# A feed-forward norm's weight moved from the tokens to the gate and up weights, and the end of the operand's stage reordered

## The chip, the cores and the metric

The kernel runs on one core of a Trainium2 chip. The core has five engines with a queue of instructions each: TensorE (PE) for matrix products, VectorE (DVE), ScalarE (ACT) and GpSimd (POOL) for everything elementwise, and SyncE (SP), whose queue issues the DMA transfers here. The metric is the device time of one execution in microseconds (us); lower is better.

## The reference

One layer of a streaming encoder for a prompt of 1024 tokens and for 8 samples of 16 new tokens (128 rows), model width 1024, all in fp32. Two groups of eight heads attend, their outputs are normed per head and projected, and then comes the part that matters here:

```python
def rmsnorm(x, g):
    xf = x.astype(jnp.float32)
    y = xf * lax.rsqrt(jnp.mean(xf * xf, axis=-1, keepdims=True) + EPS)
    return y.astype(x.dtype) * g

    x = x + mix @ w_out
    h = rmsnorm(x, g_ffn)
    x = x + (jax.nn.silu(h @ w_gate) * (h @ w_up)) @ w_down
```

`w_gate` and `w_up` are 1024 x 2816. The weight `g_ffn` has one value for each of the 1024 columns of `h`, which are the rows of `w_gate` and `w_up`, so it may be multiplied onto either.

## The kernel before, in words

Rows of tokens are held in nine tiles of 128: tiles 0 to 7 are the prompt, tile 8 the samples. Every fp32 product is done as three products of split operands: a high part (`...h`, `hi`, made by a cast on ACT) and a low part (`...l`, `lo`, what the cast left out, made by a subtraction on DVE or POOL). So each operand costs an ACT pass and a DVE or POOL pass before PE can use it.

**The operand's stage** (lines 957 to 1126) makes the feed-forward operand. For each tile, in the order 0, 4, 1, 5, 2, 6, 8, 3, 7, `lower` (L996) multiplies the second half of the mix by the output weights and adds the first half's result on DVE (L1001); `normed_halves` (L1004) squares the two halves on ACT (L1011), makes the reciprocal root (two DVE operations, L1013 and L1014, and a power on POOL, L1015) and writes the normed row `hrow`; `spread` (L1025) turns that row with eight PE transposes (L1030) and splits the result. Tiles t and t + 4 (t < 4) are combined into the seven forms B11, B21, B22, T1 to T4 of a Strassen-like product of 2x2 blocks (seven products in place of eight); tile 8 goes into `h8`, used alone in a "decode" product (`decoded`, L1064).

In `normed_halves` DVE scales the first half by the root and by the row of the norm's weight at once (L1019). The second half goes to ACT (scale, L1021) and then POOL (times the row, L1022), but for the last two tiles, where DVE does it too (`soon`). The weight's row, `g_row`, is loaded once, copied to all 128 partitions (512 KB, L126 and L978).

**The feed-forward loop** (lines 1143 to 1226) has 22 chunks, gate and up by turns, of 256 columns each. `gate_up` (L980) issues the transfer of a chunk's 1 MB of weights into one raw buffer (L141; there is only one, so a transfer waits until the last chunk's raw values are used up). `gate_up_parts` splits them in four pieces (`whi` L159 on ACT, `wlo` L105 on POOL), `sums` (L1076) makes the four sums of blocks on DVE, and `sum_parts` (L1086) splits those. These are used one chunk later. In a chunk PE first multiplies B11 (`first`, L1069); ACT copies the result into `u` (L1073) before PE goes on adding to the same bank (`product(a, ..., True)`, L1166).

**What sets the order.** A planner orders each engine's instructions from its own estimate of their times, except where the code says that an engine takes the order of the program. In this stage PE takes the program's order from the third tile on (L1100), and from the last tile on PE, ACT and DVE do (L1112), until the block's end at L1126; POOL and SP are the planner's throughout. After that all engines are the planner's, with the raw weights' casts kept behind certain splits (L1163).

The end of the stage before: at tile 3 (`j == NT - 2`) the first gate chunk is split with DVE (L1114). At the last tile (7) comes the decode product of the first chunk (L1116), then tile 3's transposes, tile 7's norm, the sums, S1's split, the first product, tile 7's transposes and forms (L1122 to L1126).

## Time and profile before

| | us |
|---|---|
| median of 3 runs | 1719.52 (1718.66 to 1720.41) |
| the profiled execution, its own time | 1712.64 |
| its span, from first to last instruction | 1710.6 |
| PE busy | 1651.7 (97%) |
| DVE busy | 1099.0 (64%) |
| ACT busy | 807.1 (47%) |
| POOL busy | 805.7 (47%) |

The profile is one execution recorded by the hardware. Each row of a timeline gives the start, the length, the engine, the source line, the operation with its output and input, and in brackets how long the engine stood before it and what released it. L12 is line 12 of the kernel; a helper's line stands for all who call it, so `L105` is every low part that is a plain subtraction. `pt` and `ps` are PE's result banks, `hrow` the normed row, `wraw` the raw weights, `u` and `sg` the loop's results. A matmul's length overlaps with the next one's start.

### The profile page before, as it was taken

How to read it: one execution, taken by the hardware profiler on the slowest of the kernel's cores; microseconds unless marked ns; L12 is line 12 of the kernel's file. 1: busy time of each engine (PE TensorE's matmuls, PEld its weight loads, DVE VectorE, ACT ScalarE, POOL GpSimd, SP SyncE). 2: the span in 40 equal slices, each digit the busy share in tenths (PEclk: the TensorE clock that was granted, in tenths of full speed). 3: DMA queues.
4: the chain of work that ended last, by engine and by line, in shares of the span. 5: the costliest groups of instructions: out<-in, count | busy, mean ns of one | idle time of the engine just before them, and what ended most of it. 6: DMA issues, size and time to landing. Idle time of an engine off the chain costs nothing.

```text
span 1710.6 us, 27738 instructions
## 1 busy us (share of the span) xinstructions
PE 1651.7 (97%) x10308; PEld 1421.3 (83%) x10308; DVE 1099.0 (64%) x1716; ACT 807.1 (47%) x1713; POOL 805.7 (47%) x652
## 2 busy tenths in 40 slices
PE   8999999989997999898989999999999999999998
PEld 7999888989996887787868888888888878878887
DVE  6111444379889666854787666666565597798875
ACT  5323545366778777643543233333332244433673
POOL 2313301277356411322345555555555379968763
PEclk9999999999998999999999999999999999999999
DMA  5847888665369885854422222222222597722222
GB/s 193 276 151 219 275 292 293 187 187 168 116 181 277 276 266 163 252 176 169 153 82 96 96 96 95 96 93 87 86 89 95 214 367 256 257 79 111 99 98 99
DMA packets 172810, 293.49 MB, mean 172 GB/s; under 512 B 16642, under 2 KB 96258, under 8 KB 170371
## 3 DMA queue, kind: packets, MB, share of 16 engines
q1 hardware_dynamic: 172674, 291.71, 52.0%
q8 instruction: 82, 1.34, 0.3%
q14 instruction: 54, 0.43, 0.1%
HBM read 204.77 MB, written 86.90 MB: 171 GB/s over the span
## 4 chain that ended last, share of the span: by engine, by line
PE 78%; DVE 7%; DMA 6%; ACT 3%; POOL 3%; issue 2%; SPq 1%; POOLq 0%; DVEq 0%; ACTq 0%
PE ps L1058 24%; PE ps L100 6%; PE ps L101 6%; PE ps L102 6%; PE pt L1321 4%; PE pt L1058 3%; PE ps L1321 3%; PE pt L610 2%; PE pt L405 2%; PE acc L468 2%; DMA v<-sv 2%; DVE keep L114 2%; PE po L634 1%; PE sdec L427 1%; PE S L579 1%
## 5 line engine op out<-in xcount | busy, mean ns | idle before, releaser
L105 POOL TENSOR_TENSOR wlo<-wraw,whi 128x512 fp32r<-128x512 f32 (+1 forms) x119 | 211.3, 1798 | 139.7 <-ACT whi L159 138.5
L100 PE MATMUL ps<-whi,hTh 128*128 128x256 f32 x576 | 167.7, 291 | 1.3 <-ACT st L267 1.3
L101 PE MATMUL ps<-wlo,hTh 128*128 128x256 f32 x576 | 164.2, 285 | 0.0
L102 PE MATMUL ps<-whi,hTl 128*128 128x256 f32 x576 | 163.7, 284 | 0.1
L159 ACT CAST whi<-wraw 128x512 fp32r<-128x512 f32 (+1 forms) x122 | 88.6, 744 | 71.4 <-PE ps L1058 28.6
L100 PEld LDWEIGHTS ps<-whi,hTh 128*128 128x128 f32 x576 | 110.4, 192 | 7.9 <-issue 5.7
L592 POOL TENSOR_TENSOR w<-w,keep 128x127 f32<-128x127 f32 (+4 forms) x64 | 78.6, 1230 | 74.8 <-DVE keep L114 64.5
L102 PEld LDWEIGHTS ps<-whi,hTl 128*128 128x128 f32 x576 | 110.4, 192 | 0.8 <-DVE hTl L105 0.4
L101 PEld LDWEIGHTS ps<-wlo,hTh 128*128 128x128 f32 x576 | 110.5, 192 | 0.2
L614 ACT CAST wth<-pt 128x512 fp32r<-128x512 f32 (+1 forms) x192 | 84.4, 466 | 44.5 <-PE pt L610 43.9
L105 DVE TENSOR_TENSOR wtl<-pt,wth 128x512 fp32r<-128x512 f32 (+1 forms) x192 | 94.1, 513 | 14.8 <-ACT wth L614 14.7
L114 DVE TENSOR_TENSOR_SCAN keep<-keep,zero 128x128 f32<-128x128 f32 (+7 forms) x64 | 101.6, 1588 | 1.7
L610 PE MATMUL pt<-ident,w 128*128 128x128 f32 x528 | 90.4, 284 | 8.5 <-DVE wtl L105 4.4
L610 PEld LDWEIGHTS pt<-ident,w 128*128 128x128 f32 x528 | 64.2, 144 | 21.6 <-DVE wtl L105 6.0
L579 PE MATMUL S<-qk 128*128 128x384 f32 (+2 forms) x192 | 71.9, 376 | 6.5 <-ACT keep L583 4.4
L633 PE MATMUL po<-wth,vk 128*128 128x256 f32 (+1 forms) x304 | 76.5, 283 | 1.5 <-DVE wtl L105 1.2
L105 POOL TENSOR_TENSOR actl<-actr,acth 128x1024 fp32r<-128x1024 f32 (+1 forms) x22 | 61.2, 2782 | 34.2 <-DMA sr<-acts 20.7
L634 PE MATMUL po<-wtl,vk 128*128 128x256 f32 (+1 forms) x304 | 73.4, 285 | 0.0
L406 DVE COPY kT<-pt 128x512 f32<-128x512 f32 x48 | 33.0, 687 | 53.4 <-PE pt L405 49.5
L101 PE MATMUL ps<-hTl,whi 128*128 128x384 f32 x192 | 65.4, 341 | 0.0
L102 PE MATMUL ps<-hTh,wlo 128*128 128x384 f32 x192 | 65.3, 340 | 0.0
L100 PE MATMUL ps<-hTh,whi 128*128 128x384 f32 x192 | 65.3, 340 | 0.0
(441 smaller groups left out, 5292.1 us busy)
## 6 DMA issues: line engine op xcount, KB each, us to landing
draw<-in_cache_sb_k SPq DMA_DIRECT2D x32, 512.0 KB, 5.7
draw<-in_cache_sb_v SPq DMA_DIRECT2D x32, 512.0 KB, 5.7
act<-sg SPq DMA_DIRECT2D x11, 1152.0 KB
actr<-act SPq DMA_DIRECT2D x22, 576.0 KB, 9.5
wraw<-in_w_in SPq DMA_DIRECT2D x11, 1024.0 KB, 8.7
wraw<-in_w_gate SPq DMA_DIRECT2D x11, 1024.0 KB, 5.5
wraw<-in_w_up SPq DMA_DIRECT2D x11, 1024.0 KB, 5.4
v<-sv SPq DMA_DIRECT2D x36, 256.0 KB, 4.7
```

The source lines that it names most:

```text
L100: T.matmul(out, lhsT=ah, rhs=bh, start=start, stop=False)
L101: T.matmul(out, lhsT=ah, rhs=bl, start=False, stop=False)
L102: T.matmul(out, lhsT=al, rhs=bh, start=False, stop=stop)
L105: return eng.tensor_tensor(out, a, hi.bitcast(F32), op=ALU.subtract)
L114: V.tensor_tensor_scan(rev, rev, zero[:, 0:1].to_broadcast([P, n - d]), keep[:, n - d : n - d + 1], op0=ALU.mult, op1=ALU.max)
L159: A.copy(h[:, o], v[:, o])
L579: T.matmul(sc, lhsT=hd["qq"][:, qs], rhs=hd["kkh"][:, kc], start=True, stop=False)
L610: T.transpose(pt[:, (c - c0) * P : (c - c0 + 1) * P], w[:, c * P : (c + 1) * P], ident)
L614: A.copy(wth[:, ks, qs], pv)
L634: T.matmul(dst, lhsT=vs, rhs=wtl[:, kb - base, c0:c1], start=False, stop=(i == nkb - 1))
L1058: T.matmul(out, lhsT=a[x][:, k], rhs=b[y][:, k], start=(not more and k == 0 and n == 0), stop=(k == 3 and n == 2), skip_group_check=more)
L1321: T.matmul(out, lhsT=a[i][:, x, m * P : (m + 1) * P], rhs=b[j][:, x], start=(not more and x == 0 and n == 0), stop=(x == 1 and n == 2), sk ...
```

## The change

The norm's weight is loaded as a column per block of 128 (`g_in`, 8 values for each partition) right behind the two small loads of `g_out`, and no longer as a row. `gate_up` multiplies it onto the raw weights in place: eight ACT operations of 128x256 behind each chunk's transfer, in front of the split and the sums. The normed row is then only the scale by the root, both halves on ACT.

At the end of the operand's stage: the first chunk's low parts are made by POOL and not DVE; tile 3's transposes come before the decode product; that product is cut into two halves, the second one behind the first chunk's second product; the first product and the copy of its result come before S1's split; tile 7's forms are made in another order (T2, T3 and T1 first, then B22 and T4). In the first chunk, the sums of the second one are moved behind the adds of the results.

```diff
+    g_in = cst.tile([P, KT], F32, name="g_in")
...
     for i, g in enumerate((g_out_sb, g_out_cb)):
         nc.sync.dma_start(g_out[:, i * 4 : i * 4 + 4], g.rearrange("o (k p) -> p (o k)", p=P))
+    nc.sync.dma_start(g_in, g_ffn.rearrange("o (k p) -> p (o k)", p=P))
...
-    g_row = load_row(xg, g_ffn[0:1, :], "grow")
 
     def gate_up(i):
-        return ch.raw(cols((w_gate, w_up)[i % 2][0], i // 2), KT, 256)
+        v = ch.raw(cols((w_gate, w_up)[i % 2][0], i // 2), KT, 256)
+        for k in range(KT):
+            A.activation(v[:, k], v[:, k], AF.Copy, scale=g_in[:, k : k + 1])
+        return v
...
-            if i == 0 or soon:
-                V.scalar_tensor_tensor(h[:, o], x[i], r[:, 0:1], g_row[:, o], op0=ALU.mult, op1=ALU.mult)
-            else:
-                A.activation(h[:, o], x[i], AF.Copy, scale=r[:, 0:1])
-                G.tensor_tensor(h[:, o], h[:, o], g_row[:, o], op=ALU.mult)
+            A.activation(h[:, o], x[i], AF.Copy, scale=r[:, 0:1])
...
         A.copy(v, q0)
-        A.copy(B22[0][:, :, s], q1)
+        if t < NP - 1:
+            A.copy(B22[0][:, :, s], q1)
         V.tensor_tensor(t1, v, p0, op=ALU.subtract)
         V.tensor_tensor(q0, q1, v, op=ALU.subtract)
         V.tensor_tensor(v, q1, t1, op=ALU.subtract)
+        if t == NP - 1:
+            A.copy(T2[0][:, :, s], v)
+            A.copy(T3[0][:, :, s], q0)
+            A.copy(T1[0][:, :, s], t1)
+            V.tensor_tensor(p1, p1, v, op=ALU.subtract)
+            sub(V, T2[1][:, :, s], v, T2[0][:, :, s])
+            sub(V, T3[1][:, :, s], q0, T3[0][:, :, s])
+            sub(G, T1[1][:, :, s], t1, T1[0][:, :, s])
+            for f, x in ((B22, q1), (T4, p1)):
+                A.copy(f[0][:, :, s], x)
+                sub(V, f[1][:, :, s], x, f[0][:, :, s])
+            return
...
-    def decoded(w, e):
-        for k in range(KT):
+    def decoded(w, e, ks=range(KT)):
+        for k in ks:
...
             if j == NT - 2:
-                w = gate_up_parts(raw, V)
-            if j == NT - 1:
-                e = decoded(w, bank(256))
+                w = gate_up_parts(raw)
             if rows:
                 spread(*rows.pop())
-            rows.append((order[j], normed_halves(order[j], j >= NT - 2)))
+            if j == NT - 1:
+                e = decoded(w, bank(256), range(4))
+            rows.append((order[j], normed_halves(order[j])))
...
         s = sums(raw)
+        a, u2 = first(w)
         S = {1: sum_parts(1, s, V)}
-        a, u2 = first(w)
         spread(*rows.pop())
...
             product(a, quarter(w, 1, 0), B21, True)
+            if not i:
+                decoded(w, e, range(4, KT))
...
                 nxt = gate_up_parts(raw)
-                s = sums(raw)
...
             V.tensor_tensor(u3, u3, d, op=ALU.add)
+            if not i:
+                s = sums(raw)
             if more:
                 S_next = {x: sum_parts(x, s) for x in (1, 2, 0)}
```

6 lines of the change are left out of this document (1 added, 5 removed).

## The prediction, made before the changed kernel was run

> **What bounds the kernel now.** I read the page's first part, then busy time by stretches, then TensorE's timeline in the stretch where it falls short.
>
> ```profile
> span 1710.6 us, 27738 instructions
> 795.00:815.00 20.00, 15.04 (x72) 11.18 (x72) 9.06 (x18) 7.64 (x15) 6.04 (x5) 0.91 0.50 165
> 815.00:850.00 35.00, 35.00 (x175) 29.11 (x174) 26.50 (x46) 19.59 (x45) 15.14 (x14) 1.00 0.47 171
> 850.00:895.00 45.00, 39.01 (x186) 30.41 (x185) 39.94 (x62) 24.67 (x53) 22.16 (x17) 0.96 0.22 70
> 895.00:1385.00 490.00, 487.44 (x2166) 402.57 (x2165) 302.92 (x357) 156.36 (x264) 258.31 (x173) 1.00 0.32 115
> 877.60:881.00 3.40, 3.40 (x10) 2.36 (x8) 3.12 (x5) 2.10 (x5) 1.40 (x2) 0.51 0.95 298
> ```
>
> The columns after the length of a stretch are the busy times of TensorE (PE), its weight loads, VectorE (DVE), ScalarE (ACT) and GpSimd (POOL), then granted clock, DMA share and GB/s. The operand's stage runs from about 807 to 895. It is full of matmuls until 850; its end, 850 to 895, has 45 − 39.01 = 6.0 us in which PE stands. Behind it the feed-forward loop runs 490 us with PE filled, while ACT is busy for 156 us (32%) and POOL for 258 us (53%). Work put on ACT there is free unless it stops something; the change can win only the 6.0 us, and 3.40 × (1 − 0.51) = 1.7 us in which PE ran at half clock. The ten holes:
>
> ```profile
> 855.25 0.65 PE L1030 MATMUL pt<-ident,hrow 128*128 128x128 f32 x4 [0.36 <-DVE hrow L1019]
> 856.97 0.66 PE L1030 MATMUL pt<-ident,hrow 128*128 128x128 f32 x4 [1.07 <-POOL hrow L1022]
> 860.85 0.63 PE L1030 MATMUL pt<-ident,hrow 128*128 128x128 f32 x4 [0.45 <-DVE hrow L1019]
> 862.04 0.63 PE L1030 MATMUL pt<-ident,hrow 128*128 128x128 f32 x4 [0.57 <-DVE B22l L105]
> 869.43 0.50 PE L1058 MATMUL ps<-B11h,whi 128*128 128x512 f32 x1 [0.24 <-ACT B11h L1036]
> 870.15 0.50 PE L1058 MATMUL ps<-B11l,whi 128*128 128x512 f32 x1 [0.22 <-DVE B11l L105]
> 873.29 1.23 PE L1030 MATMUL pt<-ident,hrow 128*128 128x128 f32 x8 [0.35 <-DVE hrow L1019]
> 876.32 0.50 PE L1058 MATMUL ps<-B21h,whi 128*128 128x512 f32 x1 [1.81 <-ACT u L1073]
> 890.51 0.50 PE L1058 MATMUL ps<-B11h,whi 128*128 128x512 f32 x1 [0.39 <-DVE dec L1185]
> 893.40 0.50 PE L1058 MATMUL ps<-T4h,whi 128*128 128x512 f32 x1 [0.54 <-DVE u L1195]
> ```
>
> In brackets: how long PE stood, and what released it. They add up to 6.00. Four are the normed rows of tiles 6, 8 and 7 (`hrow`) coming late, one is a bank, two the split of tile 3, the longest the copy of the first product (`u`), and two lie in the first chunk, behind DVE.
>
> **The change part by part.**
>
> *The norm without its row.* Removed per tile: the DVE pass that also multiplied by the row, and for seven tiles GpSimd's pass over the other half. Added: that ACT scales both halves.
>
> ```profile
> L1022 POOL TENSOR_TENSOR hrow<-hrow,row_grow 128x512 f32<-128x512 f32 x7 | 11.4, 1635 | 3.3 <-ACT hrow L1021 3.3
> L1019 DVE SCALAR_TENSOR_TENSOR hrow<-xa,r_n,row_grow 128x512 f32<-128x512 f32 x9 | 9.9, 1097 | 1.6 <-POOL r_n L1015 1.4
> L1015 POOL TENSOR_TENSOR r_n<-r_n,nhalf 128x1 f32<-128x1 f32 x9 | 5.2, 575 | 39.5 <-DVE r_n L1014 39.5
> L105 POOL TENSOR_TENSOR wlo<-wraw,whi 128x512 fp32r<-128x512 f32 x4 | 6.4, 1632 | 1.0 <-ACT whi L159 1.0
> 1409.26 1.94 ACT L1362 ACTIVATE q<-q,g_gate 128x512 f32<-128x512 f32 x3
> L1362 ACT ACTIVATE q<-q,g_gate 128x512 f32<-128x512 f32 x16 | 11.1, 720 | 18.4 <-DMA q<-in_w_ple_gate 13.3 <-POOL actl L105 5.1
> ```
>
> (Groups give count, then total and mean busy time.) L1362 is the operation of the change, a scale by a column, on 512 elements: 0.72 alone, three in 1.94, so (1.94 − 0.72)/2 = 0.61 apart. From the reciprocal root (L1015) to the whole row it took one ACT pass and then a POOL pass, 0.72 + 1.64 = 2.4 us; it will take 0.61 + 0.72 = 1.3. DVE loses 9.9 us, and the four subtractions of the first chunk's parts besides. ACT gains eleven scalings, 11 × 0.61 = 6.7 us, where it has 15 of 35 us free. So 1.1 us comes off the path of each row. Tile 6's 0.36 + 1.07 goes to nothing. PE then reaches tile 8 earlier by 1.4, and tile 8's row and bank (0.45 + 0.57) come earlier by only about as much: I leave 0.6 of the 1.02.
>
> The four `wlo` passes, now on POOL (1.63 each), stand in the queue of the root and of T1's and T2's subtractions. A root behind one of them makes its row 1.6 late. My sum has none behind one; the rival below has two.
>
> *The end of the stage.* Tile 3's transposes move ahead of the decode product, which used to cover their wait. From the rows of the holes, the twelve matmuls of a lower product take 860.85 − 0.45 − 856.97 − 0.66 = 2.8 us, and the 24 of the decode product 869.43 − 0.24 − 862.04 − 0.63 − 2.8 − 1.23 = 2.5. PE now has only the 2.8 of tile 7's lower product while tile 3's add, squares, root and two scalings (1.3) run: a new hole, 0.5, between 0 and the 2.5 that covered it. Half of the decode product now covers tile 3's split, so 0.24 + 0.22 goes. Tile 7's row keeps its length but has half a decode less ahead of it and starts earlier by as much: 0.2 instead of 0.35.
>
> ```profile
> 875.16 0.62 ACT L1088 CAST S1h<-s 128x512 fp32r<-128x512 f32 x1 [3.93 <-DVE s L1081]
> 875.69 0.58 ACT L1073 COPY u<-ps 128x512 f32<-128x512 f32 x1
> ```
>
> Here is the longest hole: the copy of `u` stood on ACT behind the cast of S1, which waited for DVE's sums. The change exchanges them; the product was ready at about 873, so the copy ends before tile 7's transposes do: 1.81 goes to 0.2. What is late next is the last tile's T2 and S2, two forms made by DVE one after another at 0.68 each. The other half of the decode product (1.3 us), and T2 and T3 being made first, lie over that; I leave 0.5, between 0 and 1.3.
>
> *The first chunk.* The next chunk's sums go behind the adds that PE waited for; 0.39 + 0.54 shrinks to 0.1. Those sums are needed only a chunk later, and the raw buffer is let go by a few us later at most, in front of a transfer that the loop has time for.
>
> Holes after: 0 + 0.6 + 0.5 + 0 + 0.2 + 0.2 + 0.5 + 0.1 = 2.1, against 6.0: −3.9. **The clock:** the half clock began 1.3 us after the hole of 1.81. With that hole gone I take the 1.7 as gone too; bounds 0 and −1.7.
>
> [...]
>
> *Scaling the weights.* Eight passes of 128x256 in every one of 22 chunks; no such row exists.
>
> ```profile
> L159 ACT CAST whi<-wraw 128x512 fp32r<-128x512 f32 x88 | 53.0, 622 | 54.1 <-PE ps L1058 28.6 <-PE pt L102 22.1 <-DMA wraw<-in_w_gate 3.4
> L159 ACT CAST whi<-wraw 128x1024 fp32r<-128x1024 f32 x34 | 35.7, 1057 | 17.3 <-PE ps L102 7.3 <-PE ps L101 5.0 <-DMA wraw<-in_w_in 3.3
> 1012.03 0.38 SPq L141 DMA_DIRECT2D wraw<-in_w_gate  x1
> 1027.70 0.59 ACT L1073 COPY u<-ps 128x512 f32<-128x512 f32 x1
> 1029.06 0.62 ACT L159 CAST whi<-wraw 128x512 fp32r<-128x512 f32 x1 [0.24 <-PE pt L102]
> 1035.15 0.38 SPq L141 DMA_DIRECT2D wraw<-in_w_up  x1
> 1044.37 1.14 ACT L159 CAST whi<-wraw 128x512 fp32r<-128x512 f32 x2
> 1052.25 0.58 ACT L1073 COPY u<-ps 128x512 f32<-128x512 f32 x1
> 1057.19 0.39 PE L1058 MATMUL ps<-B21h,whi 128*128 128x512 f32 x1
> DMA to landing us min/median/max: 5.3/5.4/5.6
> ```
>
> 512 elements more cost 1.057 − 0.622 = 0.435, so 256 fewer take 0.22 off: 0.61 − 0.22 = 0.39 apart, 8 × 0.39 + 0.1 = 3.2 us a chunk (estimate), 70 us in all. ACT goes from 32% to about 46%. For a gate chunk the transfer lands at 1012.4 + 5.4 = 1017.8 and the scalings end at 1021; the casts waited until 1029 for a matmul anyway. For an up chunk they end at 1035.5 + 5.4 + 3.2 = 1044.1, just where its casts began. Value 0, with a cover of 8 us in the one and 0.3 in the other; if the second cover is gone, POOL's passes over the parts shift by as much, and PE uses those parts only in the following chunk. The first chunk's scalings come when ACT has little to do (795 to 815: 7.6 of 20 us) or while it works on the mix that PE waits for: 0.3, bounds 0 and +3.2.
>
> *Transfers.*
>
> ```profile
> 788.75 0.79 SPq L126 DMA_DIRECT2D row_grow<-in_g_ffn  x1
> 792.00:794.00 2.00, 2.00 (x19) 1.95 (x18) 0.69 (x1) 1.60 (x2) 1.60 (x2) 1.00 0.45 175
> 13.69 3.09 SPq L141 DMA_DIRECT2D wraw<-in_w_in  x1
> 42.30 2.00 ACT L159 CAST whi<-wraw 128x1024 fp32r<-128x1024 f32 x2
> DMA to landing us min/median/max: 8.6/9.2/9.7
> ```
>
> The row's 512 KB were issued at 788.75 and the queues were under half busy by 792 to 794, so its loss does not hasten the mix rows that PE awaits in 795 to 815: 0, bound −1.3 (512 KB at 175/0.45 = 389 GB/s). The new column is as scattered as the two small loads that landed in 9.2 us (the last row). It goes ahead of a weight transfer issued at 13.69 and not used until 42.30: 0, since even 9.2 us more would be covered.
>
> **Sum:** −3.9 − 1.7 + 0.3 = −5.3 (rounded) on the profiled execution, whose own time is 1712.64 (span 1710.6). The median of the runs is 1719.52, 6.9 above it; I carry the difference over: **1714.3**. Bounds −9 and no gain at all.
>
> **Rivals.**
>
> *The holes come back on POOL.* Two roots of tiles 6, 8 and 3 fall behind a `wlo` pass, 2 × 1.6 = 3.2 given back: 1717.5. For it: POOL's order is the planner's, and the passes follow the casts of the first chunk's parts, which it may put among these very tiles. Against it: seven passes of 1.6 left that queue.
>
> *The half clock stays.* Other holes of half a microsecond remain: −3.6, 1715.9. For it: the slow stretch has a DMA share of 0.95, and that transfer comes again, so the cause may be another than the hole. Against it:
>
> ```profile
> 855.00:860.00 5.00, 3.68 (x19) 2.98 (x20) 4.16 (x8) 3.60 (x9) 3.61 (x3) 1.00 0.42 143
> ```
>
> five us with 1.3 of holes, spread out, kept the full clock; the slow stretch follows one long hole. [...]
>
> *ACT is held by the transfer, slower.* The scalings wait at the head of ACT's queue, and the casts of S, the sigmoids and the copy of `u` stand behind them; PE and POOL wait for these. L1362 shows it: six of its waits for a transfer took 13.3 us, 2.2 each. Held 2.2 + 3.2 = 5.4 us in front of a copy of `u`, that copy would be late, since PE needs it only 1057.19 − 1052.25 − 0.58 = 4.4 us after it is made. It decides from 4.4 us on. In one chunk of two, 11 × 1.0 = 11 us: 1714.3 + 11 = 1725. Against it: the scalings end 6.7 and 8 us ahead of the copies at 1027.70 and 1052.25.
>
> [...]
>
> *The change doesn't remove the wait:* the copy of `u` moves but the scalings of tile 7, now all on ACT, hold it. That is worth at most 0.6 and lies in the forecast's range.
>
> **How the numbers follow.** Forecast 0.56, POOL 0.21, half clock 0.12, held ACT 0.11. This kernel's measurement can tell about 0.2%, 3.4 us: faster is below 1716.1, slower above 1723. Forecast (all but a few hundredths) and half the clock case give faster 0.60; POOL and the rest same 0.29; the held ACT slower 0.11. Range: from all holes and the clock gone (−7.7, 1711.8, a little more for the transfers' bound) to the first scalings' +3.2 on the POOL case, 1720.7, with a little for repeats and the row's −1.3: 1711.5 to 1721.5. The likeliest case alone: 1711.8 to 1717.
>
> **What would show it.** Right: PE idle in 850 to 895 near 2 us instead of 6, no hole behind `u` L1073, clock 1.00 through 877 to 881, eight scalings of about 0.5 in each chunk with PE full from 895 to 1385. Wrong: holes released by POOL's root; the slow clock still there; PE waits in the loop behind ACT; a longer wait for the mix at 801 to 815.

## The result, and the profile after

| | before | after |
|---|---|---|
| median beside each other, us | 1718.08 (1716.00 to 1720.41, 6 runs) | 1726.55 (1723.92 to 1733.50, 6 runs) |
| profiled execution, own time | 1712.64 | 1726.37 |
| its span | 1710.6 | 1724.5 |

The ratio is 1.0064, 95% interval 1.0049 to 1.0078: slower, outside the forecast's range. Of all the executions below one, of the kernel with the column in place and chunk 1 held, took 3281.17 us and is left out of its ratio.

The page of the changed kernel: its span, the chain of work that ended last (shares by engine, then by line), and the group of the scalings (count, busy total and mean ns, then how long ACT stood before them and for what).

```profile
span 1724.5 us, 27899 instructions
PE 65%; DVE 12%; DMA 11%; ACT 6%; POOL 4%; issue 3%; SPq 1%; POOLq 0%; ACTq 0%; DVEq 0%
PE ps L1066 12%; PE ps L101 6%; PE ps L102 6%; PE ps L103 6%; PE pt L1332 5%; PE ps L1332 4%; DMA wraw<-in_w_gate 3%; ACT wraw L979 3%; DMA wraw<-in_w_up 2%; PE pt L606 2%; PE pt L401 2%; PE acc L464 2%; DMA v<-sv 2%; PE pt L1066 1%; PE sdec L423 1%
L979 ACT ACTIVATE wraw<-wraw,g_in 128x256 f32<-128x256 f32 x176 | 72.9, 496 | 122.2 <-DMA wraw<-in_w_gate 74.9
```

The same part of the page of the kernel before.

```profile
PE 78%; DVE 7%; DMA 6%; ACT 3%; POOL 3%; issue 2%; SPq 1%; POOLq 0%; DVEq 0%; ACTq 0%
PE ps L1058 24%; PE ps L100 6%; PE ps L101 6%; PE ps L102 6%; PE pt L1321 4%; PE pt L1058 3%; PE ps L1321 3%; PE pt L610 2%; PE pt L405 2%; PE acc L468 2%; DMA v<-sv 2%; DVE keep L114 2%; PE po L634 1%; PE sdec L427 1%; PE S L579 1%
```

This is the first reading to make. Before, the loop's products were 24% of the chain. Now they are 12%, and three new links stand in it: the gate transfer 3%, the scalings 3%, the up transfer 2%. The scalings' busy time, 72.9 us, is near the 70 of the estimate; what changed is that the way through the raw weights has become part of what sets the end.

Where the time went is counted in what TensorE lost. From the first transpose of a normed row on (822.7 before, 822.8 after) I add up its work in the timeline, each matmul at what one takes start to start in the undisturbed stretches of the kernel before (0.2275 us for 512 columns, 0.118 for 256, 0.07 for 128, the mean of the loop's own; those of the normed rows, 0.109 apart, are counted at 0.07 too, alike in every kernel), and take that from the time elapsed. The lost time when so much work was done:

| after work of | place | before | after | difference |
|---|---|---|---|---|
| 45 us | the last B21 products, just ahead of T2's | 10.3 | 5.0 | −5.4 |
| 65 us | first chunk | 13.2 | 14.1 | +0.9 |
| 150 us | about the fourth chunk | 13.3 | 18.8 | +5.5 |
| 500 us | the loop's end | 12.8 | 26.8 | +14.0 |

The last row is the 13.9 us of span. The medians differ by only 8.5, and the ratio's interval stands for 8.4 to 13.4: the profiled execution of the kernel before was one of its quicker ones (1712.64, median 1718.08), and with the new column's 32 bytes the way up to the stage is some 4 us shorter (means of the first experiment below). The end of the stage gained 5.4. Between 45 and 65 that is given back (+6.3), the first chunks take 4.6 more, and the steady loop, priced at nothing, 8.5. "A pair" is, below, the time from one copy of `u` to the second one after it, one gate and one up chunk: 43.77 in the kernel before, from the third pair to the end of the loop.

The holes of TensorE in the changed kernel from 850 to 945 (timeline; in brackets how long PE stood and what released it), and the granted clock there (windows: length, busy time of PE, PEld, DVE, ACT, POOL, granted clock, DMA share, GB/s).

```profile
859.26 1.27 PE L1025 MATMUL pt<-ident,hrow 128*128 128x128 f32 x8 [0.30 <-ACT hrow L1017]
863.92 1.27 PE L1025 MATMUL pt<-ident,hrow 128*128 128x128 f32 x8 [0.59 <-ACT hrow L1017]
877.27 0.49 PE L1066 MATMUL pt<-T2h,S1h 128*128 128x512 f32 x1 [2.76 <-ACT T2h L1045]
878.08 0.47 PE L1066 MATMUL pt<-T2l,S1h 128*128 128x512 f32 x1 [0.32 <-DVE T2l L106]
885.20 0.51 PE L1066 MATMUL ps<-T3h,S2l 128*128 128x512 f32 x1 [1.83 <-DVE S2l L106]
937.14 0.50 PE L1066 MATMUL ps<-T4h,whi 128*128 128x512 f32 x1 [1.46 <-DVE u L1204]
941.27 0.50 PE L1066 MATMUL ps<-B22h,S3h 128*128 128x512 f32 x1 [0.87 <-DVE u L1206]
```

```profile
850.00:895.00 45.00, 39.19 (x182) 31.06 (x181) 32.75 (x51) 30.73 (x65) 20.10 (x17) 0.92 0.20 66
878.00:882.00 4.00, 3.92 (x11) 3.14 (x12) 1.23 (x2) 4.00 (x10) 1.30 (x1) 0.61 0.00 0
886.00:889.00 3.00, 3.00 (x8) 2.33 (x8) 3.00 (x3) 0.00 (x0) 3.00 (x3) 0.50 0.00 0
```

The holes of the normed rows are 0.30 and 0.59, and the hole of 1.81 behind the copy of `u` is gone. In its place stands one of 2.76 ahead of T2's first product, one of 1.83 ahead of S2's low part, and half clock behind each. The timelines of SP and ACT show what T2 waited for:

```profile
870.29 0.38 SPq L137 DMA_DIRECT2D wraw<-in_w_up  x1
875.40 1.30 ACT L979 ACTIVATE wraw<-wraw,g_in 128x256 f32<-128x256 f32 x3 [2.95 <-DVE pt L1048]
876.61 0.60 ACT L1045 CAST T2h<-t 128x512 fp32r<-128x512 f32 x1
```

Three scalings of the second chunk's weights stand ahead of the cast of T2. The code writes them later; the planner moved them up. The row names a result of DVE (L1048) that they don't read, ready at the same moment; what they needed is their transfer, which took 5.0 from issue to landing. T2's values were there from 874.61 on (DVE's L1043), so ACT stood 0.8 for the transfer and worked 1.2 on the scalings while T2 waited. They could go there because their transfer was issued at 870.29, 6.1 us earlier than before (876.36), now that chunk 0's sums and parts let the raw tile go earlier.

And the loop. One pair, 1045 to 1090: the transfers' issues on SP, the scalings, the casts and the last readers of the raw tile on ACT, POOL and DVE.

```profile
1045.17 0.38 SPq L137 DMA_DIRECT2D wraw<-in_w_up  x1
1050.45 3.31 ACT L979 ACTIVATE wraw<-wraw,g_in 128x256 f32<-128x256 f32 x8 [4.27 <-DMA wraw<-in_w_up]
1054.70 2.30 ACT L155 CAST whi<-wraw 128x512 fp32r<-128x512 f32 x4
1056.91 6.86 POOL L106 TENSOR_TENSOR wlo<-wraw,whi 128x512 fp32r<-128x512 f32 x4
1065.94 1.78 DVE L1091 TENSOR_TENSOR s<-wraw,s 128x512 f32<-128x512 f32 x1
1067.74 0.38 SPq L137 DMA_DIRECT2D wraw<-in_w_gate  x1
1072.90 3.31 ACT L979 ACTIVATE wraw<-wraw,g_in 128x256 f32<-128x256 f32 x8 [7.28 <-DMA wraw<-in_w_gate]
1081.19 0.63 ACT L1145 ACTIVATE tmp<-u 128x512 f32<-128x512 f32 x1 [3.19 <-DVE u L1214]
1083.24 0.63 ACT L1145 ACTIVATE tmp<-u 128x512 f32<-128x512 f32 x1 [0.42 <-DVE u L1216]
1083.78 2.17 ACT L155 CAST whi<-wraw 128x512 fp32r<-128x512 f32 x4
1084.46 5.50 POOL L106 TENSOR_TENSOR wlo<-wraw,whi 128x512 fp32r<-128x512 f32 x4 [0.75 <-ACT whi L155]
1089.98 0.38 SPq L137 DMA_DIRECT2D wraw<-in_w_up  x1
```

Read it as a cycle. The gate transfer is issued at 1067.74, when the last sum (1065.94 + 1.78) has read the up weights; the up transfer at 1089.98, when the last low part (1084.46 + 5.50) has read the gate's. The way from one up transfer to the next is 44.81: two landings, 5.28 and 5.16; two sets of scalings, 3.31 each; and 27.8 of casts, low parts, sums and what they queue behind. There is one raw tile, so this is a ring, and a pair cannot be shorter than it. I call it the ring from here on. The 27.8 is not work of a fixed length. The gate's scalings end at 1076.21, but its casts start at 1083.78: ACT first does what had come to stand behind the scalings in its queue, and two sigmoids among it wait for adds to `u` on DVE (the rows of 1081.19 and 1083.24), which stand behind sums of the scaled weights. In the timelines of ACT, DVE and POOL nothing on the whole way round was released by PE.

### The profile page after: what moved, and what is told of

The parts are those of the page before. It is cut to its first block, busy times and chain, and to the rows that moved or that the text cites. A ratio compares the mean times of both kernels' runs of the same rounds, so it can differ in the third digit from the quotient of the medians.

```text
span 1724.5 us, 27899 instructions
## 1 busy us (share of the span) xinstructions
PE 1661.7 (96%) x10308; PEld 1418.5 (82%) x10308; DVE 1110.4 (64%) x1702; ACT 874.4 (51%) x1900; POOL 807.1 (47%) x648
## 4 chain that ended last, share of the span: by engine, by line
PE 65%; DVE 12%; DMA 11%; ACT 6%; POOL 4%; issue 3%; SPq 1%; POOLq 0%; ACTq 0%; DVEq 0%
PE ps L1066 12%; PE ps L101 6%; PE ps L102 6%; PE ps L103 6%; PE pt L1332 5%; PE ps L1332 4%; DMA wraw<-in_w_gate 3%; ACT wraw L979 3%; DMA wraw<-in_w_up 2%; PE pt L606 2%; PE pt L401 2%; PE acc L464 2%; DMA v<-sv 2%; PE pt L1066 1%; PE sdec L423 1%
## 5 line engine op out<-in xcount | busy, mean ns | idle before, releaser
L106 POOL TENSOR_TENSOR wlo<-wraw,whi 128x512 fp32r<-128x512 f32 (+1 forms) x123 | 216.7, 1787 | 145.7 <-ACT whi L155 144.6
L979 ACT ACTIVATE wraw<-wraw,g_in 128x256 f32<-128x256 f32 x176 | 72.9, 496 | 122.2 <-DMA wraw<-in_w_gate 74.9
L610 ACT CAST wth<-pt 128x512 fp32r<-128x512 f32 (+1 forms) x192 | 84.3, 465 | 43.8 <-PE pt L606 43.2
L106 DVE TENSOR_TENSOR wtl<-pt,wth 128x512 fp32r<-128x512 f32 (+1 forms) x192 | 94.2, 513 | 14.8 <-ACT wth L610 14.6
L155 ACT CAST whi<-wraw 128x512 fp32r<-128x512 f32 (+1 forms) x122 | 84.6, 738 | 19.6 <-DMA wraw<-in_w_in 8.6
L1090 DVE TENSOR_TENSOR s<-wraw 128x512 f32<-128x512 f32 x22 | 26.0, 1182 | 61.7 <-ACT wraw L979 34.7
```

What stands on the lines that cost most here:

```text
L106: return eng.tensor_tensor(out, a, hi.bitcast(F32), op=ALU.subtract)
L155: A.copy(h[:, o], v[:, o])
L610: A.copy(wth[:, ks, qs], pv)
L979: A.activation(v[:, k], v[:, k], AF.Copy, scale=g_in[:, k : k + 1])
```

## The experiments

Columns: the median; its ratio to the kernel before beside it; PE's lost time after 45, 65, 150 and 500 us of work, as above; and a pair in the steady loop (in brackets the least and the greatest, where they lie far apart). The expectations speak of "the stage's end" and "the loop" by three marks: first transpose of a normed row, first product of B11, first product with the down weights into `pt`. By these the kernel before has 46.7 and 493.0, the changed one 44.6 and 509.7; those two stand last.

| kernel | median | ratio (95%) | lost after 45 / 65 / 150 / 500 | a pair | stage / loop |
|---|---|---|---|---|---|
| before | – | 1 | 10.3 / 13.2 / 13.3 / 12.8 | 43.77 | 46.7 / 493.0 |
| changed | 1726.55 | 1.0064 (1.0049 to 1.0078) | 5.0 / 14.1 / 18.8 / 26.8 | 44.9 | 44.6 / 509.7 |
| changed, once more | 1727.92 | 1.0056 (1.0037 to 1.0075) | 5.1 / 14.2 / 19.6 / 27.9 | 45.0 | 44.6 / 510.6 |
| 32 unused bytes | 1718.84 | 1.0011 (1.0000 to 1.0022) | 10.5 / 13.7 / 15.0 / 19.9 | 44.41 | 47.1 / 499.8 |
| changed, 64 bytes | 1735.03 | 1.0100 (1.0083 to 1.0118) | 4.7 / 14.1 / 20.5 / 32.5 | 45.4 | 44.1 / 515.4 |
| old order, weights scaled | 1719.78 | 1.0017 (1.0006 to 1.0027) | 6.7 / 8.4 / 10.8 / 19.1 | 44.9 | 44.5 / 501.9 |
| new order, row on the tokens | 1723.50 | 1.0035 (1.0020 to 1.0050) | 10.5 / 12.4 / 14.7 / 14.2 | 43.77 | 50.2 / 491.2 |
| changed, column in place | 1734.30 | 1.0113 (1.0091 to 1.0135) | 4.7 / 14.0 / 20.3 / 31.4 | 45.3 | 44.1 / 514.2 |
| ... and chunk 1 held | 1731.43 | 1.0086 (1.0061 to 1.0111) | 4.5 / 6.1 / 14.6 / 25.5 | 45.3 | 44.2 / 508.4 |
| old order, column in place | 1728.44 | 1.0077 (1.0056 to 1.0098) | 6.2 / 7.8 / 11.8 / 23.2 | 45.3 | 44.0 / 506.1 |
| changed, no scalings | 1714.25 | 0.9994 (0.9977 to 1.0011) | 4.5 / 11.1 / 11.1 / 10.8 | 43.77 | 43.9 / 493.6 |
| column in place, sums held | 1736.89 | 1.0117 (1.0090 to 1.0144) | 4.7 / 12.3 / 16.9 / 34.0 | 45.9 (44.3 to 47.2) | 44.1 / 516.8 |
| ... and chunk 1 held | 1736.30 | 1.0107 (1.0091 to 1.0124) | 4.5 / 6.1 / 15.4 / 33.5 | 45.9 (44.4 to 47.2) | 44.1 / 516.6 |
| both held, column as changed | 1724.56 | 1.0046 (1.0027 to 1.0065) | 5.1 / 7.1 / 16.0 / 29.8 | 45.0 | 44.6 / 512.5 |
| half the scalings | 1721.80 | 1.0022 (1.0008 to 1.0037) | 4.5 / 10.0 / 15.7 / 15.4 | 43.77 | 43.9 / 498.2 |
| new order, scalings on DVE | 1725.45 | 1.0050 (1.0034 to 1.0066) | 4.5 / 13.3 / 18.9 / 19.8 | 43.9 | 44.2 / 502.7 |
| old order, scalings on DVE | 1726.02 | 1.0052 (1.0031 to 1.0072) | 6.2 / 10.9 / 20.3 / 20.9 | 43.9 | 43.9 / 503.9 |
| old order, ACT and DVE | 1716.78 | 1.0005 (0.9993 to 1.0017) | 6.0 / 8.0 / 13.2 / 12.7 | 43.77 | 44.0 / 495.9 |
| new order, ACT and DVE, chunk 1 held | 1715.58 | 0.9992 (0.9979 to 1.0004) | 4.5 / 6.3 / 12.5 / 12.2 | 43.77 | 44.0 / 494.9 |
| changed, chunk 1 held | 1723.03 | 1.0034 (1.0019 to 1.0050) | 5.2 / 7.1 / 14.3 / 23.1 | 45.0 | 44.7 / 505.7 |

The stretch up to the operand's stage, which no kernel changes but for 32 bytes of place, ended between 819.0 and 832.1 in these profiles; so spans and profiled times are not compared below, only lost times and medians. "In place" is explained where it first comes up.

### Does the place of the column matter, by itself?

In the loop of the changed kernel the products of the T forms with the sums took longer one by one. First suspect: the column's 32 bytes for each partition move everything that is laid out behind the constants. The kernel before, with 32 bytes that nobody reads:

```diff
     g_out = cst.tile([P, KT], F32, name="g_out")
+    pad = cst.tile([P, KT], F32, name="pad")
+    V.memset(pad, 0.0)
```

> The kernel before, with nothing added but 32 unused bytes per partition, allocated where the change puts its column and set to zero once. Theory 1 (place in memory): all that is allocated on the left behind it moves by 32 bytes, and the products of the loop whose one operand lies left (T1, T2, T3, B22) and whose other lies right (S0 to S3) start 0.234 us apart and not 0.227, median length 396 ns and not 389: 96 in two chunks, 0.7 us, some 7 us over the loop, so about 1725 and 0.4% slower. Rival (the slower pace comes from ScalarE's added writes to the same memory, or from the run): 389 ns, loop as before, ratio 1.000.

And the changed kernel with 64 bytes in place of 32:

```diff
-    g_in = cst.tile([P, KT], F32, name="g_in")
+    g_in = cst.tile([P, 16], F32, name="g_in")[:, :KT]
```

> The changed kernel, its column given 64 bytes per partition and not 32. Theory 1 (place in memory): the offset that the kernel before had comes back (modulo 64), the mixed products go back to 389 ns, 7 us less than the changed kernel, about 1719. Rival (ScalarE's work slows them, or 32 bytes more move them as far again): 396 ns or another length, about 1726.

One line's instructions, of the kernel before, with 32 unused bytes, and as changed (least, median and greatest ns; first and last start):

```profile
L1058 PE MATMUL pt<-T2h,S1h x88: 389/389/562, 880.6 to 1344.1; 128*128 128x512 f32 x88
```

```profile
L1060 PE MATMUL pt<-T2h,S1h x88: 389/395/495, 877.4 to 1348.5; 128*128 128x512 f32 x88
```

```profile
L1066 PE MATMUL pt<-T2h,S1h x88: 393/396/628, 877.3 to 1358.5; 128*128 128x512 f32 x88
```

The place matters: 32 unused bytes alone give the longer products, a pair of 44.41 and 7.1 us more lost by the loop's end (19.9 against 12.8). 64 bytes restore the pace in part (392 for these products, 388 for those of T2h with S1l), and that kernel was slower still.

The median rose by only 0.11% (0.00 to 0.22), some 2 us. The profiles of all the kernels of the table show where the rest is: with the 32 bytes the way up to the stage is shorter. The first transpose of a normed row starts at 819.0 to 825.6 in the six kernels that have them (mean 822.4) and at 822.7 to 832.1 in the thirteen that have the old place (mean 826.8; with 64 bytes 826.9). It shows early: the 901st matmul, the same in all of them, starts at 134.0 to 134.5 in the six and at 135.0 to 135.6 in the thirteen. So by these means the place gives back ahead of the stage some 4 of the 7 us that it takes in the loop, and the profile of the kernel before, at 822.7, is the earliest of its thirteen. What in that stretch gets faster, no run shows.

### The two halves of the change, apart

The weights scaled, but all in the order of before:

```diff
-        return ch.raw(cols((w_gate, w_up)[i % 2][0], i // 2), KT, 256)
+        v = ch.raw(cols((w_gate, w_up)[i % 2][0], i // 2), KT, 256)
+        for k in range(KT):
+            A.activation(v[:, k], v[:, k], AF.Copy, scale=g_in[:, k : k + 1])
+        return v
...
+            A.activation(h[:, o], x[i], AF.Copy, scale=r[:, 0:1])
```

> The norm's weight on the gate and up weights alone; the end of the stage in the order of before, first parts on VectorE, decode product whole. Theory 2 (ScalarE held by the transfers): the scalings wait for the weights as in the changed kernel (about 120 us in all, holes behind VectorE's additions in the first four chunks and 0.3 us in each second chunk after), so the loss is all here: 1725 to 1732. Rival (the new order is what loses): 1719 or less.

The new order, with the row on the tokens as before:

```diff
-        for k in range(KT):
-            A.activation(v[:, k], v[:, k], AF.Copy, scale=g_in[:, k : k + 1])
...
-            A.activation(h[:, o], x[i], AF.Copy, scale=r[:, 0:1])
+            if i == 0 or soon:
+                V.scalar_tensor_tensor(h[:, o], x[i], r[:, 0:1], g_row[:, o], op0=ALU.mult, op1=ALU.mult)
+            else:
+                A.activation(h[:, o], x[i], AF.Copy, scale=r[:, 0:1])
+                G.tensor_tensor(h[:, o], h[:, o], g_row[:, o], op=ALU.mult)
```

> The new order at the end of the stage alone; the norm keeps its row, no scaling of weights, no column. Theory 2: no loss in the loop (458 us from the first copy of u to the last but for its start), T2 not delayed by scalings, so the end of the stage wins 3 to 5 us: about 1714. Rival (the new order puts T2 and S2 late by itself): holes of 2.8 and 1.8 us ahead of T2 and S2 stay, 1718 to 1722.

TensorE's holes at the end of the stage, first with the weights scaled in the old order, then with the new order alone (timelines).

```profile
873.03 1.27 PE L1030 MATMUL pt<-ident,hrow 128*128 128x128 f32 x8 [0.61 <-ACT hrow L1022]
874.63 0.50 PE L1058 MATMUL ps<-B21h,whi 128*128 128x512 f32 x1 [0.33 <-ACT u L1073]
879.19 0.50 PE L1058 MATMUL pt<-T2l,S1h 128*128 128x512 f32 x1 [0.87 <-POOL T2l L106]
```

```profile
862.00 0.66 PE L1031 MATMUL pt<-ident,hrow 128*128 128x128 f32 x4 [1.76 <-DVE hrow L1020]
864.35 1.11 PE L1031 MATMUL pt<-ident,hrow 128*128 128x128 f32 x4 [1.70 <-POOL hrow L1023]
874.63 1.32 PE L1031 MATMUL pt<-ident,hrow 128*128 128x128 f32 x8 [1.89 <-DVE hrow L1020]
```

And POOL's timeline of the latter: a root (L1016) behind two of the low parts.

```profile
857.12 2.54 POOL L105 TENSOR_TENSOR wlo<-wraw,whi 128x512 fp32r<-128x512 f32 x2 [2.57 <-ACT whi L159]
859.62 0.54 POOL L1016 TENSOR_TENSOR r_n<-r_n,nhalf 128x1 f32<-128x1 f32 x1
```

Scaling the weights, without any new order, already takes the hole behind `u` from 1.81 to 0.33 and the lost time after 45 us of work from 10.3 to 6.7: with the row off the tokens, tile 7's rows and the queue behind them are sooner done. The new order on top of it gives 1.7 more (5.0). Alone it gives nothing (10.5): its low parts stand on POOL where the rows also need POOL, which is the prediction's first rival, in a kernel that still has the row. The median of this kernel is 0.35% above the kernel before, more than the 1.4 us of lost time by the loop's end; the rest lies outside this stretch and was not taken apart.

Behind the stage the two don't add up. The scalings in the old order lose 10.7 from 65 us on (19.1 − 8.4), of which the 32 bytes account for 6.2 (19.9 − 13.7); the new order alone 1.8. Together it is 12.7, after 9.1 between 45 and 65, where these two lose 1.7 and 1.9.

### The column in the place of other bytes

If the place costs some 7 us, giving the column bytes that the constants held already should win it back. The order of every queue stays as in the changed kernel.

```diff
-    nhalf = cst.tile([P, 16], F32, name="nhalf")
+    nhalf = cst.tile([P, KT], F32, name="nhalf")
...
-        G.tensor_tensor(r[:, :n], r[:, :n], nhalf[:, :n], op=ALU.pow)
+        G.tensor_tensor(r[:, :n], r[:, :n], nhalf[:, 0:1].to_broadcast([P, n]), op=ALU.pow)
```

> The changed kernel with its column of weights in 32 bytes that the constants held already (the table of exponents is cut from 16 columns to 8, and its one reader of 16 takes one column repeated), so that everything behind the constants lies where it lay in the kernel before; the order of every queue is that of the changed kernel. Placement theory: the products of T2, T3, T1 with sums of weights are back at 389 ns in the median (396 in the changed kernel), the loop falls by the 6.8 us that 32 unused bytes cost the kernel before, from 509.7 to about 503, and the time falls to about 1720 to 1724. Hoisting theory: the hole ahead of T2's first product (2.76 us) and the half clock behind it stay as they are, so the stage's end stays at 44.6 and the time stays above the kernel before. Rival (the pace comes from the scalings' traffic in the loop and not from the place): 395 ns and the loop at 510.

The same, with chunk 1's scalings held behind the last cast of chunk 0's sums:

```diff
-    def gate_up(i):
+    def gate_up(i, after=()):
         v = ch.raw(cols((w_gate, w_up)[i % 2][0], i // 2), KT, 256)
+        with ExitStack() as held:
+            for m in after:
+                held.enter_context(tc.issue_after(m))
...
-                raw = gate_up(1)
+                raw = gate_up(1, [marks[0].ins])
```

> As the run before it (column in place), and chunk 1's scalings are held behind the last cast of chunk 0's sums, so on ACT they come behind T2, T3, T1, B22, T4 and the sums. Hoisting theory: the holes ahead of T2h (2.76), S2l (1.83), and the two ahead of u in the loop (1.46 and 0.87) go, with most of the half clock behind them (3.2 us of lost time): 7 to 9 us less than the run before it, of which a late start of chunk 1 (its casts come some 8 us later) may take 1 to 3 back; loop about 495, time 1711 to 1716. Rival (the scalings' traffic on ACT is what costs, wherever it stands): no more than 2 us below the run before it.

The old order with the column in place:

> The weights scaled in the order of before, with the column in place. Placement theory: 389 ns, the loop of the run without the column in place (501.9) less 6.8, so about 495, and a time about 2.5 us under that run's 1719.8: about 1717, or within 0.2% of the kernel before. Stage's end 44.5. Rival (scaling in the loop costs by itself): the loop stays at 500 or above.

And the changed kernel without scalings and column (the norm's weight is left out altogether):

> The changed kernel without the 176 scalings and without their column (the norm's weight is left out altogether); the order of the queues is otherwise the planner's, with chunk 1's first three casts ahead of T2's. If the scalings cost nothing beside the hoist and the placement: T2's hole is about 1 us (three casts of 0.58 in place of the scalings), the loop 492 to 495, stage's end 43 to 45, time 1710 to 1714. If the standing of ACT in the loop (120 us behind the weights' transfers) costs the path: 3 us or more below the run with the scalings held behind T2's forms.

The pace came back, 389 ns, and all three scaled kernels got slower by it, not faster (1.0113 against 1.0064 for the changed kernel; the other two are "chunk 1 held" and the old order). The placement theory has the pace right and the time wrong. About half of the loss lies ahead of the stage, by the 4.4 between the means above; the other half, 4.6, is in the lost time (31.4 against 26.8). The pairs tell why: 45.3 with the column in place, whatever the order, although the products alone need 43.77; the kernel without scalings is at 43.77. Something other than PE sets the loop. The waits of PE in 960 to 1340, column in place (us in total, times, longest):

```profile
PE ps L1066 <- DVE u L1206: 9.3, 8, 1.4
```

Eight waits of 1.2 us, one in nearly every pair, for the add that frees a bank of the results. With the column as changed the slower products fill that time: there the same wait is short (1.5 in all), and the pair is 44.9.

The kernel without scalings says a second thing. With no scaling at all the change gains 5.8 by 45 us of work and keeps 2.0 of it (10.8 against 12.8): 3.35 us are lost ahead of T2h there too, now behind three casts of chunk 1's weights, for whose transfer ACT stood 3.20. Its median is not measurably below the kernel before.

### Which queue?

First the changed kernel again, beside the next three:

> The changed kernel once more, beside the next three. The run with the column in place came out at 1734.3, 7.8 above the changed kernel's 1726.6 with the same order in every queue, where the placement theory wanted 5 less. If that difference is the kernels' own, this run is at 1725 to 1728 with a pair of chunks each 44.9 us; if it is the chip's, this run is at 1732 to 1736.

It was at 1727.92, so the 1734.30 with the column in place is the kernel's own. The add that PE waits for stands on DVE behind a sum that waits for the scalings. So I held the sums behind that add:

```diff
-                s = sums(raw)
+                with tc.issue_after(freed):
+                    s = sums(raw)
...
-            V.tensor_tensor(u3, u3, d, op=ALU.add)
+            freed = V.tensor_tensor(u3, u3, d, op=ALU.add).ins
             if not i:
-                s = sums(raw)
+                with tc.issue_after(freed):
+                    s = sums(raw)
```

> The changed kernel with the column in place and the four DVE sums of a raw chunk held behind the add that frees the third product's bank two chunks earlier (u3 + d), in whose way the first of them stands on DVE, waiting for the scalings. DVE theory: it is the sums at the head of DVE's queue that make the add late, 1.2 us in each pair of chunks; with them behind it a pair takes 43.77 us again (the pace of the matrix products alone, as in the run without scalings, against 45.3 with the column in place), ten pairs give back 15 us, loop about 499, time about 1719; T2's hole (3.0) stays. Rival, as in the prediction's slower case (the scalings at the head of ACT's queue hold up casts and copies): a pair stays at 45 or above. Rival (the transfer, the scalings and the casts are a ring that is too long by itself): a pair stays at 45, and another wait appears ahead of the products.

> As the run before it, and chunk 1's scalings held behind the last cast of chunk 0's sums. If both theories hold (the sums on DVE cost 15 us in the loop; the scalings ahead of T2h cost its hole of 3.0, S2l's of 1.2 and half clock): stage's end 44, loop 491 to 494, time 1711 to 1716, at or below the kernel before. If only the hoist was a cost, it stays near the 1731.4 of the run with the scalings alone held.

> As the run before it, with the column where the change put it (32 bytes more in the constants). Placement theory: with the waits gone the products' pace sets the loop, so 395 ns and 44.41 us a pair, as in the kernel before with 32 unused bytes: loop 498 to 500, time 5 to 7 above the run before it. If the place matters only for the scaled loop's waits: both runs the same.

The DVE theory fell: a pair is 45.9 in the mean (44.3 to 47.2), no shorter than the 45.3 without the hold, and the times don't fall. PE's timeline with the column in place and the sums held has another add of the results in place of the first:

```profile
1028.04 0.50 PE L1066 MATMUL ps<-T4h,whi 128*128 128x512 f32 x1 [1.12 <-DVE u L1205]
1073.18 0.50 PE L1066 MATMUL ps<-T4h,whi 128*128 128x512 f32 x1 [1.07 <-DVE u L1205]
```

A wait that moves when its releaser is moved, at a period no shorter, points past it to something that goes round. (It does not prove it alone: the held sums also let the raw tile go later.) That is the ring through the raw tile, the second rival of that run's expectation. The first one, that ACT's queue is held, expects the same period; it is not excluded by this, since what stands behind the scalings on ACT is a part of that way round. The last of the three keeps the placement out of it: with 32 bytes more the pair is 45.0, not 44.41, since the products' pace isn't what binds.

### A ring has a threshold

If the ring binds, its price is not in proportion to ACT's work: shorten it below 43.77, and all of the price is gone. Every other scaling left out (so half of the weights' rows go without the norm's weight), column in place:

```diff
-        for k in range(KT):
+        for k in range(0, KT, 2):
             A.activation(v[:, k], v[:, k], AF.Copy, scale=g_in[:, k : k + 1])
```

> The changed kernel with the column in place (32 bytes that the constants held already), and only every other of the eight scalings of a chunk (half of the weights' rows go without the norm's weight). Ring theory: the way from a raw tile's transfer to the next one through it is 3.3 us shorter in a pair (4 x 0.41 less, twice), 45.3 - 3.3 = 42.0, below the products' 43.77, so a pair takes 43.8 us, the loop is 15 us shorter than the 514.2 of the run with all eight: about 498, time 1717 to 1721. Rival (the price goes with ACT's time in scalings): half of the 1.5 us remains, a pair at 44.5, loop 506.

The transfers' issues with half the scalings (SP's timeline):

```profile
1038.71 0.38 SPq L137 DMA_DIRECT2D wraw<-in_w_up  x1
1060.44 0.38 SPq L137 DMA_DIRECT2D wraw<-in_w_gate  x1
1082.26 0.38 SPq L137 DMA_DIRECT2D wraw<-in_w_up  x1
```

and its page's chain, by line:

```profile
PE ps L1066 23%; PE ps L101 7%; PE ps L102 6%; PE ps L103 6%; PE pt L1332 4%; PE pt L1066 3%; PE ps L1332 3%; PE pt L606 3%; PE pt L401 2%; PE acc L464 2%; DMA v<-sv 2%; PE po L630 2%; PE po L629 1%; PE sdec L423 1%; PE S L575 1%
```

A pair is 43.77 within a hundredth in more than half of the loop and 43.8 in the mean (the in-between of 44.5, by the rival, does not occur); the products are back at 23% of the chain, and transfer and scalings have left it. From 150 to 500 us of work it loses nothing (15.7 and 15.4), where the kernel with all eight loses 11.1 (20.3 to 31.4). So the price has a threshold, which a cost in proportion to the scalings has not. The time is 1721.8, a little above the expected upper end; the hole ahead of T2h (3.05) and the first chunks' waits are still there (+2.6 against the kernel before by the loop's end).

### All the scalings, but a shorter ring

A second raw tile should open the ring, but no run has one. The scalings were moved, in both orders, column in place, first to DVE:

```diff
-            A.activation(v[:, k], v[:, k], AF.Copy, scale=g_in[:, k : k + 1])
+            V.tensor_scalar(v[:, k], v[:, k], g_in[:, k : k + 1], None, op0=ALU.mult)
```

> The changed kernel with the column in place and the eight scalings on DVE in place of ACT. Ring theory: if one takes 0.25 to 0.4 us (a DVE multiplication of 128x256 from PSUM takes 0.42), they end 2 us or less after the landing plus nothing on ACT, the ring is at 42 to 44 and a pair at 43.8 to 44; nothing stands ahead of T2h on ACT but casts; loop 493 to 498, time 1712 to 1719. Rival (any engine that waits at its head for the transfer delays what is behind it): the adds to u on DVE come late, a pair at 45 or above, time as the run with ACT, 1734.

> The order of the kernel before, weights scaled on DVE, column in place. Ring theory: a pair at 43.8, loop 493 to 496, stage's end 44: time 1712 to 1716, 1 to 4 below the kernel before. Rival as in the run before it: 1725 to 1728, as with the scalings on ACT.

Better than ACT, and neither theory's number. On DVE's timeline the eight took 4.29 and 3.23 us, as long as on ACT and not the 2 that I had assumed, and the adds to `u` stand behind them:

```profile
1099.67 4.29 DVE L979 TENSOR_SCALAR wraw<-wraw,g_in 128x256 f32<-128x256 f32 x8 [2.44 <-DMA wraw<-in_w_up]
1103.88 0.67 DVE L1204 TENSOR_TENSOR u<-u,ps 128x512 f32<-128x512 f32 x1
1120.77 3.23 DVE L979 TENSOR_SCALAR wraw<-wraw,g_in 128x256 f32<-128x256 f32 x8 [1.85 <-DMA wraw<-in_w_gate]
```

The steady loop is as short as the ring theory wanted it, with 0.9 and 0.6 us lost from 150 to 500 and not 11, but not by its sum: 7.5 us of scalings stand in this pair where ACT's 6.6 were too many. On DVE they leave ACT's queue free (the cast of S0, which follows the gate's scalings at 1076.59 in the changed kernel, starts at 1120.89 here, beside them). So what the scalings hold up on ACT counts in the ring too; how much of it, no run takes apart. The times are not as it wanted, since the first chunks lose 14 us, in holes of up to 6.8, while DVE, which has the most to do there, stands for a transfer with T2's and S2's low parts and the adds behind it. That is the rival's mechanism, in another place than it expected. With the scalings on both engines:

```diff
+            if k % 2:
+                V.tensor_scalar(v[:, k], v[:, k], g_in[:, k : k + 1], None, op0=ALU.mult)
+            else:
+                A.activation(v[:, k], v[:, k], AF.Copy, scale=g_in[:, k : k + 1])
```

> The order of the kernel before; of a chunk's eight scalings ACT takes the even ones and DVE the odd ones side by side; column in place. Ring theory: four scalings end 1.7 us (ACT, 0.41 each) to 2.2 us (DVE, 0.54) after the landing, the way through the raw tile is 2.2 to 3.3 us shorter in a pair, 42.0 to 43.1, so a pair takes 43.8, loop 494 to 498, time 1714 to 1719. Rival (DVE waiting at its head for the transfer makes u late, as in the runs with all eight on DVE): a pair at 44.2 and the first chunks with holes of 3 to 7 us, time 1724.

> The new order with the scalings spread as in the run before it, and chunk 1's held behind the last forms of chunk 0's sums. Ring theory: a pair at 43.8; no T2 hole beyond 0.8, loop 493 to 497, stage's end 44: time 1712 to 1718. If the new order is worth anything beyond the old one, this run is below the run before it. Rival: as there, 1724.

With the new order, chunk 1 held: a stretch of the stage's end and the loop (windows), then ACT's and DVE's share of one chunk side by side (timeline).

```profile
850.00:895.00 45.00, 42.91 (x220) 35.11 (x219) 35.44 (x61) 32.87 (x68) 22.78 (x19) 1.00 0.29 94
895.00:1340.00 445.00, 440.95 (x1954) 364.21 (x1953) 282.91 (x403) 169.50 (x323) 243.73 (x162) 1.00 0.27 94
```

```profile
1064.61 1.71 ACT L985 ACTIVATE wraw<-wraw,g_in 128x256 f32<-128x256 f32 x4 [3.46 <-DMA wraw<-in_w_gate]
1064.55 1.20 DVE L983 TENSOR_SCALAR wraw<-wraw,g_in 128x256 f32<-128x256 f32 x4 [1.94 <-DMA wraw<-in_w_gate]
```

All 176 scalings are done, a pair takes 43.77, and nothing is lost from 150 us on. The median is 15.9 below nearly the same kernel with all scalings on ACT (1715.58 against 1731.43, ratios 0.9992 and 1.0086). Both orders end level with the kernel before: 0.9992 (0.9979 to 1.0004) and 1.0005 (0.9993 to 1.0017). What the stage's end gained, the first chunks took (6.3 to 12.5, two holes of 1.38 and 2.67 for the adds to `u` among it). No version of the change was found that is measurably faster than the kernel before.

### The hoisted scalings of the second chunk

The changed kernel, the column where it was, with only chunk 1's scalings held (the edit shown above):

> The changed kernel as it is, but chunk 1's scalings held behind the last cast of chunk 0's sums (nothing else, the column where the change put it). Hoisting theory: the hole ahead of T2h (2.76) falls to 0.8, S2l's (1.83) and the half clock (3.2 of lost time) go, while chunk 1 starts later: 2 to 5 us below the changed kernel, 1722 to 1725. Rival (the loop's ring eats what the start gives, since chunk 1's transfer comes later): the same time as the changed kernel, 1726 to 1728.

```profile
878.16 0.49 PE L1069 MATMUL pt<-T2h,S1h 128*128 128x512 f32 x1 [0.81 <-ACT T2h L1048]
```

The hole ahead of T2 is 0.81 in place of 2.76, S2's is gone, and so is the half clock (granted clock 1.00 from 850 to 895, against 0.92): 7.0 us less lost by 65 us of work. Half of it is lost again in the first chunks, among others in waits of 1.40 and 1.15 for an add to `u` and its copy (3.7 less by 500). The median is 3.5 lower, 1723.03, but the intervals of the ratios just touch (1.0019 to 1.0050, 1.0049 to 1.0078), so it is the profile more than the runs that makes the hoist a second, smaller price.

## Why the prediction was wrong

*The holes of the normed rows* were right: tile 8's 0.30 and the new one ahead of tile 3 0.59 (0.6 and 0.5 predicted), tile 6's, tile 3's split, tile 7's and the `u` copy's gone (0.2 predicted for each of the last two). The lost time there fell by 5.4, more than the 3.6 that these terms make (5.1 to 1.5): they went to 0.9, and in the kernel before most of the half clock after 877.5 lies ahead of this mark too. The first chunk's term was right as well: its holes of 0.39 and 0.54 are gone, and the next transfer was issued 1.9 later (894.70, before 892.81). But the gain at `u`, the largest, was put down to the order of two ACT instructions where most of it belongs to the norm: in the old order, with the rows free of DVE's and POOL's multiplication, the hole was 0.33 already.

*"T2 and S2 are late next: 0.5, between 0 and 1.3"* failed: 2.76 + 0.32 + 1.83. The step counted only the two subtractions in T2's way. What it left out is that the planner may put work of the next chunk ahead of T2's cast, and that this change brings such work that early, by letting the raw tile go 6.1 us earlier and by giving ACT eight operations on it. Held back, T2's hole is 0.81 + 0.32, near the upper bound.

*The clock, −1.7,* failed with it. The step put the fall down to the long hole ahead of it, and here that fits: from 850 to 895 the granted clock was 1.00 where there was no long one (the run with chunk 1 held, both split runs), and in the changed kernel it was 0.61 and 0.50 behind 2.76 and 1.83. But the length of one hole does not tell whether the clock falls (last section).

*"Scaling the weights: value 0, with a cover of 8 us in the one and 0.3 in the other"* is the step that decided. The duration was right: 3.31 a chunk against 3.2. The reading of the cover was wrong. I asked of each chunk alone whether its casts would still come in time, and let a late low part pass because "PE uses those parts only in the following chunk". But casts, low parts and sums also free the one raw tile, and the next transfer waits for that. A delay there is not absorbed by a following chunk, it is carried round. The question was not the cover in a chunk but the length of the ring against the pair's 43.77, and the rows quoted held most of it: transfer, release and next transfer. In place the ring is 45.2 with two sets of 3.3, so 38.6 without them (estimate): room for 5.1, where 6.6 were put in. The estimate takes all the rest as fixed, and the runs on DVE, with 7.5 in a pair of 43.9, show that it isn't. What the steady loop lost by this step is 8.5 where the prediction has 0.

*The placement* was in no term. In the scaled kernel it worked both ways: products of 44.41 for a pair in place of 43.77, and a ring of 44.9 in place of 45.3, with a way up to the stage some 4 us shorter.

*The rivals.* "ACT is held by the transfer, slower" gave 1725 with a chance of 0.11, and the time was 1726.55. Its number was nearly that of the run, by luck, since its place was not: no copy of `u` waits in the steady loop. Its mechanism does show, ahead of T2 and inside the ring, where what stands behind the scalings on ACT comes late. But ACT's standing for the transfers (122 us in all) is not the cost: in the run with half the scalings it still stands 92.0, with a pair of 43.77. "The holes come back on POOL" exists, but in the kernel that keeps the row (1.70 behind POOL); in the changed one the rows no longer need POOL's product. "The half clock stays" had the outcome by another cause.

*The sum.* The +14.0 divide so: the stage's end −5.4; the hoist of chunk 1's scalings +7.0 by 65 us of work, of which 3.3 come back behind it; the steady loop (150 to 500) +8.5; and some 7 in the first chunks. In the steady loop, ring and place aren't separate prices, since slow products and waits cover each other: the place alone costs 5.4 there (15.0 to 19.9, before 13.3 to 12.8), the ring alone 11.6 (20.3 to 31.4). The 7 of the first chunks (7.1 to 14.3 with chunk 1 held, where the kernel before loses nothing) show waits for the adds to `u` and for its copy, but no run takes these apart.

## What to carry to other kernels

Before work is put between a transfer and the first use of its data, write down the whole cycle of the buffer that it lands in (issue, landing, the new work, what then stands behind it in its engine's queue, every reader that frees the buffer, next issue) and compare it with the period of the loop; with one buffer, cover in each chunk is not enough. A wait that only moves when its releaser is moved points to such a cycle; taking half of the new work away tells it from a cost in proportion. And where a planner orders the queues, new work that is ready early can go ahead of what the bound engine needs next.

## What the runs showed of the hardware

*The half clock.* In the kernel before the granted clock was 0.51 from 877.6 to 881, behind the hole of 1.81 that ends at 876.32; in the changed kernel 0.61 from 878 to 882 and 0.50 from 886 to 889, behind those of 2.76 and 1.83. A hole of such a length did not always bring it. With 32 unused bytes the same hole, 1.81 ahead of 874.19, had products 0.23 us apart behind it, the pace of the undisturbed stretches, and still had them at 881.00, 881.24 and 881.47. So had, in the old order with the scalings on ACT and DVE, one of 2.72 ahead of 935.28 (939.04, 939.27, 939.49). What decides, no run here shows.

*The pace of matmuls by place.* With everything behind the constants 32 bytes further on in each partition, the products of the T forms with the sums took 395 ns in the median instead of 389, those of B11 with the weights 389 as before. With 64 bytes T2h took 392 with S1h and 388 with S1l. Why, no run here shows.

*Transfers by place.* With the same 32 bytes the loop's gate transfers landed after 5.1 us in the median, and after 5.5 in the kernel before. The first of these rows is the kernel before, the second the one with 32 unused bytes (transfers of 960 to 1340: count, KB, median us from issue to landing):

```profile
wraw<-in_w_gate SPq DMA_DIRECT2D x8, 1024.0 KB, 5.5
```

```profile
wraw<-in_w_gate SPq DMA_DIRECT2D x8, 1024.0 KB, 5.1
```

In the changed kernel the scalings begin 5.28 and 5.16 after the issues quoted above, with the column in place 5.49 and 5.36 after theirs. Both differences together are 0.41 of the 0.42 by which its ring is longer (45.23 against 44.81).

*A scaling by a column on DVE* took 0.40 to 0.54 us for 128x256 with eight in a row (3.23 and 4.29 for the eight), against 0.41 on ACT (3.31); four beside ACT's took 1.20, 0.30 each, while ACT's four took 1.71, 0.43 each.
